# Asking for raw weight tiles a pair ahead in a Strassen-form MLP, and preparing the second product's first blocks in the last pair

## The chip, the cores and the metric

One Trainium2 chip, one core. The metric is device time in microseconds, the time of one execution of the whole kernel. Before the change it is 2197.11 us, the median of three runs (2195.40 to 2198.02).

## The reference

A trunk of two residual mixers (an even and an odd one), each followed by a squared-ReLU MLP, and a last RMSNorm, all in float32, for 1024 tokens of width 1024, with an MLP width of 4096. The change touches the two MLPs alone:

```python
def rmsnorm(x, g):
    xf = x.astype(F32)
    y = xf * lax.rsqrt(jnp.mean(xf * xf, axis=-1, keepdims=True) + EPS)
    return (y * g.astype(F32)).astype(x.dtype)

def sq_relu_mlp(h, w1, w2):
    u = jax.nn.relu(h @ w1)
    return (u * u) @ w2

def reference(x, ...):
    for layer in range(DEPTH):
        ...
        x = x + sq_relu_mlp(rmsnorm(x, norm_mlp[layer]), w_mlp1[layer], w_mlp2[layer])
    return rmsnorm(x, final_norm)
```

## The kernel before

**Precision.** TensorE multiplies reduced float32. Each float32 operand is therefore cut into a high half, a cast by ScalarE (L122), and a low half, the rest, by VectorE (L130), and each product of two blocks is three matmuls: high by high, high by low, low by high. A weight block with its halves is a tile `wb` (1024 columns: 512 high, 512 low); an activation block is `hb`, and in the second product `ub`.

**The first product, h @ w1.** The MLP width is cut into 16 pairs p of two column blocks. A pair needs two raw weight tiles (128 x 1024, 512 KB each), `raw(p, 0)` and `raw(p, 1)`, loaded by SyncE (DMA at L304). The 2 x 2 block product of a pair is computed in Strassen's form (Winograd's variant): 7 products of 12 matmuls (L371, all in `product`) in place of 8. The weight side has the blocks A11, A12, A22 (quarters of raw tiles) and S1 to S4 (sums of quarters, made by GpSimd, L323 to L342); the activation side has B11, B21, B22, t2, t3, T1 and t4 (in `nb.T`, prepared once for each layer by the norm object, from the residual tiles X). A11 needs raw(p, 0) alone, A12 in the first product too, A22 and S1 raw(p, 1), the others both. In what follows a product is named by its pair and activation block: 9t3 is S3 of pair 9 by t3. A11 goes with B11, A12 with B21, A22 with t4, S1 with T1, S2 with t2, S3 with t3, S4 with B22.

**Evacuation.** `head` and `head2` take the products with B11 and B21 out of a PSUM bank (ScalarE, L389, L394, L395), `rest` the other five (VectorE, L400 to L429, and squared ReLU on ScalarE, L375 and L376). The results and their sums for the second product are spilled to DRAM by `put` (SyncE, L382) and read back for the second product at L468. For pairs 14 and 15 (TAIL) the four results are put as they are, without the sums.

**Order of the pairs.** The B blocks of the first token half are ready before those of the second, so pairs 0 to 5 (NS = 6) first do only B11 and B21, from raw(p, 0) alone, while the norm of the second half is worked out: the sum of squares over partitions (L220), the factor on VectorE, its broadcast by TensorE (L231), the scale of X (L1514) and the t and T blocks (`late`, L1526 to L1541, with low halves at L130 and, negated, at L279). Then come the other five products of pairs 0 to 5, whose raw tiles are loaded a second time (both of them, named 16 + p), and then pairs 6 to 15 in full.

**Queues and tiles.** All DMAs are issued by SyncE, in its program order: a DMA whose tile isn't free or whose data isn't ready holds all behind it. A generator (`w_stream`) prepares the weight blocks; the class `Ahead` runs it W_AHEAD = 3 blocks beyond the one in use, and a raw tile is asked for when its first block is prepared. The order of instructions on each engine isn't the source's: the tile framework plans all of them before the kernel is built, and what it decided is shown below in rows. Raw tiles, X, the hb blocks, sums, evacuated halves and reloads share one pool of 41 tiles of 4 KB a partition; `wb` tiles have a pool of eight, four of which are held all through an MLP by weights of the mixer and the tail.

**The second product, u @ w2,** works in three groups of pairs (L484), again with seven products, on blocks from the same generator (raw tiles of w2) and from `t_stream` (reloads `ut`, L468). X is read back at L489 for the residual.

Of the kernel before, what the change touches and what calls it, by code (L numbers as in the profile page):

```python
# [46 lines left out]
class Trunk:  # L47
# [239 lines left out]
            return [x[:, s] for x in two for s in (slice(0, N2), slice(N2, S))]  # L287
        return [self.PB("q"), self.PB("q"), self.PA("q"), self.PA("q")]

    def w_stream(self, l, order, second):  # L290


        nc, a = self.nc, self.a
# [48 lines left out]
                    add(x, x, blk(p, 0, 1), op=ALU.add)  # L342
            return self.block("wb", x)

        for p, b in order:
            yield prep(p, b)

    def first_stream(self, l):

        start = range(NS)  # L350
        order = [x for p in start for x in [(p, "A11")] + [(p - 1, "A12")] * (p > 0)] + [(NS - 1, "A12")]
        order += [(NF // 2 + p, b) for p in start for b in ("S2", "S3", "S1", "A22", "S4")]
        order += [(p, b) for p in range(NS, NF // 2) for b in ("A11", "S2", "S3", "S1", "A12", "A22", "S4")]
        return Ahead(self.w_stream(l, order, False), W_AHEAD)

    def mlp(self, l, nb, nxt, dram):
        nc = self.nc
        dma = nc.sync.dma_start
        V = nc.vector
        NP = NF // 2  # L360
        start = range(NS)
        stream = nb.stream
# [15 lines left out]
        spill = {}  # L378

        def put(p, k, x):  # L380
            d = self.dr.tile([P, N2], F32, tag=f"{dram}{p}{k}", name=f"{dram}{p}{k}")
            dma(d, x)  # L382
            spill[p, k] = d
# [8 lines left out]
        def head2(p, ps, u11):  # L392
            product(ps, nb.T["B21"], False, True)
            nc.scalar.activation(u11, ps, AF.Relu)  # L394
            nc.scalar.activation(u11, u11, AF.Square)  # L395
            put(p, "B11", u11)

        def rest(p, b, c, d, t1, u11, second=None):
# [9 lines left out]
            if second is not None:  # L408
                second()
# [19 lines left out]
            V.tensor_tensor(x4, u21, x2, op=ALU.add)  # L429
            put(p, "t4", x4)  # L430


        early = {}
        for p in start:
# [12 lines left out]
        k = 0  # L447
        for p in start:
            bk = self.banks(k)
            k = 1 - k  # L450
            rest(p, *bk[:3], *early[p][:2])
        for p in range(NS, NP):
            a, b, c, d = self.banks(k)
            k = 1 - k
            t1, u11 = head(p, a)
            rest(p, b, c, d, t1, u11, lambda: head2(p, a, u11))


        products = (("A11", "B11"), ("S1", "T1"), ("A12", "B21"), ("S4", "B22"), ("S3", "t3"), ("S2", "t2"),
                    ("A22", "t4"))  # L460
        seq = [(g, i, p) for g in range(len(GROUPS)) for i in range(7) for p in GROUPS[g]]
        stream = Ahead(self.w_stream(l, [(p, products[i][0]) for g, i, p in seq], True), W_AHEAD)

        def t_stream():
            for g, i, p in seq:
                name = products[i][1]
                x = self.H2("ut", "ut")
                dma(x, spill[p, name])  # L468
                yield self.block("ub", x, neg=(name == "B22"))

        tin = Ahead(t_stream(), W_AHEAD)
        X = [self.G("X") for _ in range(NC)]
        done = nxt(X)
        acc = [self.H2("acv", "acv") for _ in range(4)]
# [1 line left out]

        def second(ps, pairs, first, last):
            for j, p in enumerate(pairs):
                w, x = stream.take(), tin.take()
                for m in range(4):  # L480
                    cs = slice(m * P, (m + 1) * P)
                    lo = slice(N2 + m * P, N2 + (m + 1) * P)
                    for i, (a, b) in enumerate(((w[:, cs], x[:, :N2]), (w[:, cs], x[:, N2:]), (w[:, lo], x[:, :N2]))):
                        nc.tensor.matmul(ps[m], a, b, start=(first and j == 0 and i == 0),  # L484
                                         stop=(j == len(pairs) - 1 and i == 2), skip_group_check=True)
# [5 lines left out]
        for g, pairs in enumerate(GROUPS):  # L491
# [32 lines left out]
            k = 1 - k  # L524
# [1131 lines left out]
GROUPS = (range(0, 5), range(5, 10), range(10, 14))  # L1656
# [5 lines left out]


W_AHEAD = 3

G_BUFS = 41
W_BUFS = 8
# [128 lines left out]
```

## Time and profile before

| | before |
|---|---|
| device time, median of 3 | 2197.11 us (2195.40 to 2198.02) |
| device time of the profiled execution | 2195.6 us |
| its span, first to last instruction | 2193.8 us |
| mean granted clock of TensorE | 0.98 |
| ScalarE busy | 1056.5 us (48%) |
| GpSimd busy | 812.4 us (37%) |
| matmuls of the first product, L371 | 2688, 637.9 us busy, 60.8 us idle before them |
| matmuls of the second product, L484 | 2352, 540.0 us busy, 8.2 us idle before them |

All numbers of the trace are of the profiled execution, in microseconds from its start. In a row of a group, `out<-in` names the tiles without their numbers; behind the bar stand busy time, the mean of one in ns, and the idle time of the engine just before, with what ended most of it. In a row of a timeline stand start, length, engine, line, operation, tiles, count, and in brackets the idle time before it and what ended that. In a list of waits stand the engine and line, what it waited for, the sum in us, the number of waits and the longest. The first product's pairs lie at about 307 to 669 us in the first layer and at 1500 to 1861 us in the second.

### The profile page before, as it was taken

What the parts mean: (1) busy time and instruction counts of PE and PEld (TensorE: products, weight loads), DVE (VectorE), ACT (ScalarE), POOL (GpSimd) and SP (SyncE); (2) the same over time, 40 slices, a digit from 0 to 9 for tenths busy, and PEclk for the clock granted to TensorE, in tenths of its full rate; (3) what the DMA queues carried; (4) which work ended last, traced back from release to release, by engine and by line L of the source; (5) the groups of instructions that cost most, each with busy time, mean ns of one, the idle gap of its engine ahead of it and who ended that gap; (6) DMA issues with size and microseconds to landing.
All of it is one profiled execution on the core that took longest, in us unless ns stands there. A gap on an engine that the chain in (4) does not pass through costs nothing. (4 is left out here: it accounts for less than half of the span.)

```text
span 2193.8 us, 27305 instructions
## 1 busy us (share of the span) xinstructions
PE 2060.6 (94%) x9600; PEld 1687.3 (77%) x9600; DVE 1536.4 (70%) x2365; ACT 1056.5 (48%) x1853; POOL 812.4 (37%) x635
## 2 busy tenths in 40 slices
PE   7999998999999999999997999898999999999997
PEld 5877776677777888888785998786777777788887
DVE  7688757665556877775898888717665555877964
ACT  5247645344444544340565777734544444443423
POOL 4133222232225142242558775462332221523414
PEclk9999998999999999999999999999999999999998
DMA  5630032443447635122112000243343444754402
GB/s 173 158 121 20 20 130 101 164 168 120 158 158 279 209 98 183 58 100 74 34 33 59 11 16 16 77 149 140 110 163 139 159 149 168 264 192 146 143 29 78
DMA packets 115546, 261.34 MB, mean 119 GB/s; under 512 B 19664, under 2 KB 21840, under 8 KB 115408
## 3 DMA queue, kind: packets, MB, share of 16 engines
q1 hardware_dynamic: 115408, 259.59, 35.2%
q8 instruction: 75, 1.23, 0.2%
q14 instruction: 63, 0.52, 0.1%
HBM read 178.28 MB, written 72.35 MB: 114 GB/s over the span
## 5 line engine op out<-in xcount | busy, mean ns | idle before, releaser
L371 PE MATMUL q<-hb,wb 128*128 128x512 f32 x2688 | 637.9, 396 | 60.8 <-ACT wb L122 28.4
L371 PEld LDWEIGHTS q<-hb,wb 128*128 128x128 f32 x2688 | 504.9, 190 | 192.8 <-ACT wb L122 44.8
L484 PE MATMUL q<-ub,wb 128*128 128x512 f32 x2352 | 540.0, 391 | 8.2 <-ACT wb L122 4.6
L484 PEld LDWEIGHTS q<-ub,wb 128*128 128x128 f32 x2352 | 442.8, 189 | 104.8 <-ACT wb L122 6.2
L130 DVE TENSOR_TENSOR wb<-raw,wb 128x512 fp32r<-128x512 f32 x268 | 230.3, 866 | 93.0 <-ACT wb L122 91.9
L122 ACT CAST wb<-raw 128x512 fp32r<-128x512 f32 x268 | 163.7, 618 | 189.9 <-PE q L371 84.3
L327 POOL TENSOR_TENSOR sum<-raw 128x512 f32<-128x512 f32 x32 | 42.1, 1315 | 435.7 <-DMA raw<-in_w_dram 307.2
L130 DVE TENSOR_TENSOR ub<-ut,ub 128x512 fp32r<-128x512 f32 x168 | 137.5, 831 | 71.4 <-ACT ub L122 70.9
L122 ACT CAST ub<-ut 128x512 fp32r<-128x512 f32 x168 | 101.3, 618 | 148.8 <-DVE wb L130 18.3
L130 DVE TENSOR_TENSOR wb<-sum,wb 128x512 fp32r<-128x512 f32 x152 | 127.7, 842 | 38.3 <-ACT wb L122 37.2
L122 ACT CAST wb<-sum 128x512 fp32r<-128x512 f32 x152 | 93.6, 618 | 106.9 <-PE q L371 44.2
L185 PE MATMUL z<-Hh,wh 128*128 128x512 f32 x328 | 129.8, 400 | 9.8 <-ACT wh L122 8.6
L185 PE MATMUL z<-Hl,wh 128*128 128x512 f32 x328 | 130.2, 397 | 3.3 <-DVE Hl L1457 3.1
L245 POOL TENSOR_TENSOR acc<-acc,sq 128x512 f32<-128x512 f32 (+1 forms) x62 | 84.4, 1364 | 126.4 <-ACT sq L244 124.5
L185 PE MATMUL z<-Hh,wl 128*128 128x512 f32 x328 | 129.5, 395 | 0.6 <-DVE wl L130 0.6
L323 POOL TENSOR_TENSOR sum<-raw,raw 128x512 f32<-128x512 f32 x28 | 41.4, 1486 | 209.1 <-DMA raw<-in_w_dram 203.1
L1110 PE MATMUL cav<-cpT,VS 128*128 128x256 f32 x512 | 101.9, 303 | 5.0 <-DVE cpT L1340 2.5
L122 ACT CAST wh<-raw 128x1024 fp32r<-128x1024 f32 (+1 forms) x49 | 49.7, 1015 | 108.9 <-PE z L185 39.4
L1320 PE MATMUL ms<-Kt,Qt 128*128 128x512 f32 (+1 forms) x384 | 99.8, 396 | 2.2 <-ACT e L1327 1.4
L185 PE MATMUL op<-yh,wh 128*128 128x512 f32 x252 | 99.7, 397 | 1.4 <-DVE ya L873 0.9
L185 PE MATMUL op<-yl,wh 128*128 128x512 f32 x252 | 98.8, 393 | 0.0
L185 PE MATMUL op<-yh,wl 128*128 128x512 f32 x252 | 97.9, 393 | 0.0
(343 smaller groups left out, 3798.6 us busy)
## 6 DMA issues: line engine op xcount, KB each, us to landing
raw<-in_w_dram SPq DMA_DIRECT2D x140, 512.0 KB, 4.5
xm<-X SPq DMA_DIRECT2D x32, 256.0 KB, 2.0
X<-xm SPq DMA_DIRECT2D x16, 512.0 KB, 7.0
raw<-in_o_w_out_dram SPq DMA_DIRECT2D x16, 512.0 KB, 3.6
raw<-in_o_w_in_dram SPq DMA_DIRECT2D x11, 512.0 KB, 3.5
raw<-in_e_w_in_dram SPq DMA_DIRECT2D x10, 512.0 KB, 4.9
X<-in_x_dram SPq DMA_DIRECT2D x16, 256.0 KB, 5.7
raw<-in_e_w_out_dram SPq DMA_DIRECT2D x8, 512.0 KB, 3.5
```

Source lines behind the costliest of these rows:

```text
L122: self.nc.scalar.copy(out, x)
L130: e.tensor_tensor(out, x, y, op=ALU.subtract)
L185: self.nc.tensor.matmul(ps, l, r, start=(first and i == 0), stop=(last and i == n - 1))
L245: (eng or nc.gpsimd).tensor_tensor(acc, acc, sq, op=ALU.add)
L323: add(x, blk(p, 1, 0), blk(p, 1, 1), op=ALU.add)
L327: add(s1, blk(p, 1, 0), blk(p, 1, 1), op=ALU.add)
L371: nc.tensor.matmul(ps, a, b, start=(first and c == 0 and i == 0), stop=(c == 3 and i == 2), skip_group_check=True)
L484: nc.tensor.matmul(ps[m], a, b, start=(first and j == 0 and i == 0), stop=(j == len(pairs) - 1 and i == 2), skip_group_check=True)
L1110: nc.tensor.matmul(ACC[0][:, (p % 2) * 256:(p % 2 + 1) * 256], VS[h][:, kb * P:(kb + 1) * P], pp[:, t * N2 + ii * 256:t * N2 + (ii + 1) * ...
L1320: nc.tensor.matmul(ps[:, s], l[rows, qs], r[rows, s], start=(i == 0), stop=(i == 2))
```

## The change

`w_stream` has a new argument `look`. Before it prepares block k, it now asks for the raw tiles that blocks k to k + look need; for the first product look is LOOK = 7, the number of blocks of a pair, and for the second it is 0. The generators of the second product's weight blocks and of its reloads are set up ahead of the pairs, and `turn`, which takes the place of `head2` in pairs 6 to 15, fills both when pair 15 has done its B21. Nothing else is changed. From `product` on, lines stand 5 lines lower in the new file, and from the second product on 12 lower.

```diff
@@ -287,7 +287,7 @@
             return [x[:, s] for x in two for s in (slice(0, N2), slice(N2, S))]
         return [self.PB("q"), self.PB("q"), self.PA("q"), self.PA("q")]
 
-    def w_stream(self, l, order, second):
+    def w_stream(self, l, order, second, look=0):
 
 
         nc, a = self.nc, self.a
@@ -342,7 +342,12 @@
                     add(x, x, blk(p, 0, 1), op=ALU.add)
             return self.block("wb", x)
 
-        for p, b in order:
+        uses = {"A11": (0,), "A12": (1,) if second else (0,), "A22": (1,), "S1": (0, 1) if second else (1,),
+                "S2": (0, 1), "S3": (0,) if second else (0, 1), "S4": (0, 1)}
+        for k, (p, b) in enumerate(order):
+            for q, c in order[k:k + look + 1]:
+                for i in uses[c]:
+                    raw(q, i)
             yield prep(p, b)
 
     def first_stream(self, l):
@@ -351,7 +356,7 @@
         order = [x for p in start for x in [(p, "A11")] + [(p - 1, "A12")] * (p > 0)] + [(NS - 1, "A12")]
         order += [(NF // 2 + p, b) for p in start for b in ("S2", "S3", "S1", "A22", "S4")]
         order += [(p, b) for p in range(NS, NF // 2) for b in ("A11", "S2", "S3", "S1", "A12", "A22", "S4")]
-        return Ahead(self.w_stream(l, order, False), W_AHEAD)
+        return Ahead(self.w_stream(l, order, False, LOOK), W_AHEAD)
 
     def mlp(self, l, nb, nxt, dram):
         nc = self.nc
@@ -429,6 +434,26 @@
             V.tensor_tensor(x4, u21, x2, op=ALU.add)
             put(p, "t4", x4)
 
+        products = (("A11", "B11"), ("S1", "T1"), ("A12", "B21"), ("S4", "B22"), ("S3", "t3"), ("S2", "t2"),
+                    ("A22", "t4"))
+        seq = [(g, i, p) for g in range(len(GROUPS)) for i in range(7) for p in GROUPS[g]]
+        stream2 = Ahead(self.w_stream(l, [(p, products[i][0]) for g, i, p in seq], True), W_AHEAD)
+
+        def t_stream():
+            for g, i, p in seq:
+                name = products[i][1]
+                x = self.H2("ut", "ut")
+                dma(x, spill[p, name])
+                yield self.block("ub", x, neg=(name == "B22"))
+
+        tin = Ahead(t_stream(), W_AHEAD)
+
+        def turn(p, a, u11):
+            head2(p, a, u11)
+            if p == NP - 1:
+                stream2.fill()
+                tin.fill()
+
 
         early = {}
         for p in start:
@@ -453,22 +478,9 @@
             a, b, c, d = self.banks(k)
             k = 1 - k
             t1, u11 = head(p, a)
-            rest(p, b, c, d, t1, u11, lambda: head2(p, a, u11))
-
-
-        products = (("A11", "B11"), ("S1", "T1"), ("A12", "B21"), ("S4", "B22"), ("S3", "t3"), ("S2", "t2"),
-                    ("A22", "t4"))
-        seq = [(g, i, p) for g in range(len(GROUPS)) for i in range(7) for p in GROUPS[g]]
-        stream = Ahead(self.w_stream(l, [(p, products[i][0]) for g, i, p in seq], True), W_AHEAD)
-
-        def t_stream():
-            for g, i, p in seq:
-                name = products[i][1]
-                x = self.H2("ut", "ut")
-                dma(x, spill[p, name])
-                yield self.block("ub", x, neg=(name == "B22"))
-
-        tin = Ahead(t_stream(), W_AHEAD)
+            rest(p, b, c, d, t1, u11, lambda: turn(p, a, u11))
+
+
         X = [self.G("X") for _ in range(NC)]
         done = nxt(X)
         acc = [self.H2("acv", "acv") for _ in range(4)]
@@ -476,7 +488,7 @@
 
         def second(ps, pairs, first, last):
             for j, p in enumerate(pairs):
-                w, x = stream.take(), tin.take()
+                w, x = stream2.take(), tin.take()
                 for m in range(4):
                     cs = slice(m * P, (m + 1) * P)
                     lo = slice(N2 + m * P, N2 + (m + 1) * P)
@@ -1662,6 +1674,7 @@
 
 
 W_AHEAD = 3
+LOOK = 7
 
 G_BUFS = 41
 W_BUFS = 8
```

The instructions of each engine are the same before and after; their order and the slots of their tiles differ. First SyncE at the start of the first layer's MLP, before (`raw` are raw tiles of w1, `xm0` the spill of X, `ut0_0B11` the put of pair 0's B11; the last two raws belong to pairs 3 and 4):

```order
L304 DMA raw_580_2863<-in_w1_dram 128x1024
L304 DMA raw_582_2868<-in_w1_dram 128x1024
L304 DMA raw_585_2876<-in_w1_dram 128x1024
L1491 DMA xm0_91<-X_235_1238 128x512
L1491 DMA xm0_91<-X_234_1237 128x512
L1491 DMA xm0_91<-X_236_1239 128x512
L382 DMA ut0_0B11_3040<-t1_599_2959 128x512
L382 DMA ut0_1B11_3094<-t1_607_2991 128x512
L304 DMA raw_611_3021<-in_w1_dram 128x1024
L304 DMA raw_619_3075<-in_w1_dram 128x1024
```

And after (the first six raws are those of pairs 0 to 5 in their order, the last one is the first of pair 0's second loading):

```order
L304 DMA raw_580_2863<-in_w1_dram 128x1024
L304 DMA raw_581_2865<-in_w1_dram 128x1024
L304 DMA raw_582_2867<-in_w1_dram 128x1024
L304 DMA raw_583_2869<-in_w1_dram 128x1024
L304 DMA raw_584_2871<-in_w1_dram 128x1024
L304 DMA raw_587_2879<-in_w1_dram 128x1024
L1503 DMA xm0_91<-X_235_1238 128x512
L1503 DMA xm0_91<-X_234_1237 128x512
L1503 DMA xm0_91<-X_236_1239 128x512
L387 DMA ut0_0B11_3048<-t1_602_2965 128x512
L387 DMA ut0_1B11_3100<-t1_610_2997 128x512
L304 DMA raw_614_3027<-in_w1_dram 128x1024
```

The raw tiles of pairs 3, 4 and 5, raw_583, raw_584 and raw_587, have moved from behind the put of pair 1's B11 to ahead of the last spills of X.

Next TensorE in the same place, before: the last rows of pair 2's B11, the sum of squares (`ss`) with its broadcast (`ident`, `rr`), then 1B21 (wb_608), 3B11 (wb_612) and 4B11 (wb_620), each of four rows with three matmuls:

```order
L371 MATMUL q_614_3049<-hb_588_2886,wb_586_2878 128x512 x3
L220 MATMUL ss_600_2973<-ones_88,acc_563_2758 128x1 x4
L231 MATMUL q_606_2990<-ident_83,rr_605_2988 128x128 x4
L371 MATMUL q_606_2990<-hb_590_2907,wb_608_2992 128x512 x3
L371 MATMUL q_606_2990<-hb_593_2929,wb_608_2992 128x512 x3
L371 MATMUL q_606_2990<-hb_596_2951,wb_608_2992 128x512 x3
L371 MATMUL q_606_2990<-hb_597_2955,wb_608_2992 128x512 x3
L371 MATMUL q_614_3049<-hb_576_2838,wb_612_3023 128x512 x3
L371 MATMUL q_614_3049<-hb_577_2842,wb_612_3023 128x512 x3
L371 MATMUL q_614_3049<-hb_587_2882,wb_612_3023 128x512 x3
L371 MATMUL q_614_3049<-hb_588_2886,wb_612_3023 128x512 x3
L371 MATMUL q_630_3157<-hb_576_2838,wb_620_3077 128x512 x3
```

And after:

```order
L376 MATMUL q_618_3057<-hb_591_2892,wb_589_2884 128x512 x3
L220 MATMUL ss_603_2979<-ones_88,acc_563_2758 128x1 x4
L376 MATMUL q_632_3161<-hb_576_2838,wb_623_3083 128x512 x3
L376 MATMUL q_632_3161<-hb_577_2842,wb_623_3083 128x512 x3
L376 MATMUL q_632_3161<-hb_590_2888,wb_623_3083 128x512 x3
L376 MATMUL q_632_3161<-hb_591_2892,wb_623_3083 128x512 x3
L231 MATMUL q_609_2996<-ident_83,rr_608_2994 128x128 x4
L376 MATMUL q_609_2996<-hb_593_2913,wb_611_2998 128x512 x3
L376 MATMUL q_609_2996<-hb_596_2935,wb_611_2998 128x512 x3
L376 MATMUL q_609_2996<-hb_599_2957,wb_611_2998 128x512 x3
L376 MATMUL q_609_2996<-hb_600_2961,wb_611_2998 128x512 x3
L376 MATMUL q_644_3222<-hb_576_2838,wb_629_3134 128x512 x3
```

The product 4B11 (wb_623) has moved up between the sum of squares and the broadcast, and 5B11 (wb_629) now comes next after 1B21 (wb_611). In the second layer the broadcast keeps its place ahead of that product.

Last TensorE in the later pairs, before: pair 9's t3 (wb_787), t2 (wb_786) and B21 (wb_794):

```order
L371 MATMUL q_791_4461<-hb_624_3121,wb_787_4428 128x512 x2
L371 MATMUL q_790_4460<-hb_610_3018,wb_786_4407 128x512 x3
L371 MATMUL q_790_4460<-hb_613_3046,wb_786_4407 128x512 x3
L371 MATMUL q_790_4460<-hb_618_3072,wb_786_4407 128x512 x3
L371 MATMUL q_790_4460<-hb_621_3100,wb_786_4407 128x512 x3
L371 MATMUL q_791_4461<-hb_624_3121,wb_787_4428 128x512
L371 MATMUL q_791_4461<-hb_625_3125,wb_787_4428 128x512 x3
L371 MATMUL q_791_4461<-hb_628_3150,wb_787_4428 128x512 x3
L371 MATMUL q_791_4461<-hb_629_3154,wb_787_4428 128x512 x3
L371 MATMUL q_790_4460<-hb_590_2907,wb_794_4479 128x512 x3
L371 MATMUL q_790_4460<-hb_593_2929,wb_794_4479 128x512 x3
```

And after, t3 (wb_789), t2 (wb_788), B21 (wb_796):

```order
L376 MATMUL q_793_4465<-hb_627_3127,wb_789_4432 128x512 x3
L376 MATMUL q_793_4465<-hb_628_3131,wb_789_4432 128x512 x3
L376 MATMUL q_793_4465<-hb_630_3154,wb_789_4432 128x512 x3
L376 MATMUL q_793_4465<-hb_631_3158,wb_789_4432 128x512 x3
L376 MATMUL q_792_4464<-hb_613_3024,wb_788_4411 128x512 x3
L376 MATMUL q_792_4464<-hb_617_3054,wb_788_4411 128x512 x3
L376 MATMUL q_792_4464<-hb_622_3080,wb_788_4411 128x512 x3
L376 MATMUL q_792_4464<-hb_624_3106,wb_788_4411 128x512 x3
L376 MATMUL q_792_4464<-hb_593_2913,wb_796_4483 128x512 x3
L376 MATMUL q_792_4464<-hb_596_2935,wb_796_4483 128x512 x3
```

The product t2 no longer stands inside t3 but behind it, directly ahead of B21. The same holds for the other odd pairs from 9 to 13. On SyncE the two raws that a pair asks for stand where they stood, but they are those of the next pair. At the boundary from the first product to the second the order on SyncE is the same before and after.

## Prediction

> **What bounds the kernel now.** I read the page first, then the list of waits of TensorE, then its timeline where those waits lie, and last the engine or queue that ended each of them.
>
> ```profile
> PE 2060.6 (94%) x9600; PEld 1687.3 (77%) x9600; DVE 1536.4 (70%) x2365; ACT 1056.5 (48%) x1853; POOL 812.4 (37%) x635
> L371 PE MATMUL q<-hb,wb 128*128 128x512 f32 x2688 | 637.9, 396 | 60.8 <-ACT wb L122 28.4
> L327 POOL TENSOR_TENSOR sum<-raw 128x512 f32<-128x512 f32 x32 | 42.1, 1315 | 435.7 <-DMA raw<-in_w_dram 307.2
> raw<-in_w_dram SPq DMA_DIRECT2D x140, 512.0 KB, 4.5
> ```
>
> TensorE is busy 94% of the span, and the change gives it neither more nor fewer matmuls. So the whole question is idle time of TensorE. The matmuls of the first product (L371) have 60.8 us of it over the two layers. A raw weight tile lands 4.5 us after its issue, and GpSimd, whose sums of raw tiles are the head of the preparation (L327), spends 307.2 us waiting for such tiles. That wait costs only where it reaches TensorE:
>
> ```profile
> PE q L371 <- ACT wb L122: 28.4, 14, 8.3
> PE q L371 <- DVE wb L130: 16.6, 17, 3.1
> PE q L371 <- DVE u L403: 6.6, 8, 0.9
> PE q L371 <- DVE t L400: 3.5, 4, 0.9
> ```
>
> 45 of the 60.8 us are waits for a prepared weight block (high half by ScalarE, low half by VectorE). The other 10 are evacuations (L400, L403), which no weight load explains. Where they lie, in TensorE's timeline of the first layer (start, length, matmuls, idle before):
>
> ```profile
> 328.43 1.43 PE L231 MATMUL q<-ident,rr 128*128 128x128 f32 x8 [1.59 <-DVE rr L211]
> 330.54 5.49 PE L371 MATMUL q<-hb,wb 128*128 128x512 f32 x12 [0.67 <-ACT RB L235]
> 342.44 1.22 PE L371 MATMUL q<-hb,wb 128*128 128x512 f32 x2 [6.41 <-ACT wb L122]
> 346.20 28.84 PE L371 MATMUL q<-hb,wb 128*128 128x512 f32 x118 [2.55 <-DVE wb L130]
> ...
> 393.05 6.32 PE L371 MATMUL q<-hb,wb 128*128 128x512 f32 x26 [0.88 <-DVE u L403]
> ...
> 455.21 32.88 PE L371 MATMUL q<-hb,wb 128*128 128x512 f32 x144 [0.88 <-DVE u L403]
> ```
>
> There are three kinds of place: one large hole at the start (342 to 346 us), a broken stretch in pairs 1 to 5 (375 to 461 us), and single waits later. The undisturbed row at 455.21 gives the unit: 144 matmuls in 32.88 us, 0.229 us each, **2.75 us for a product of 12**.
>
> **The start.** SyncE, ScalarE, then the second layer on TensorE:
>
> ```profile
> 337.35 0.32 SPq L382 DMA_DIRECT2D ut_1B<-t  x1
> 337.76 8.62 SPq L304 DMA_DIRECT2D raw<-in_w_dram  x5
> ```
>
> ```profile
> 341.76 1.14 ACT L122 CAST wb<-raw 128x512 fp32r<-128x512 f32 x2 [0.50 <-DMA raw<-in_w_dram]
> ```
>
> ```profile
> 1532.46 1.22 PE L371 MATMUL q<-hb,wb 128*128 128x512 f32 x2 [8.28 <-ACT wb L122]
> 1536.83 21.23 PE L371 MATMUL q<-hb,wb 128*128 128x512 f32 x84 [3.15 <-DVE wb L130]
> ```
>
> SyncE issues in order. The raw tiles of the next pairs stand behind the spill of 1B11, which can't leave before 337.35, so they are issued from 337.76 and the first cast starts at 341.76, when its tile has come. TensorE's idle time is 6.41 + 2.55 = 8.96 us here and 8.28 + 3.15 = 11.43 us in the second layer. In the new order these raws stand ahead of the X spills, well before that put, and their tiles lie on slots long dead. So this wait goes. **What is late next is VectorE**, which carries the norm and the halves of the activations:
>
> ```profile
> 330.52 5.39 DVE L1514 SCALAR_TENSOR_TENSOR X<-X,cols,RB 128x512 f32<-128x512 f32 x8 [2.24 <-ACT RB L235]
> 335.83 2.49 DVE L1526 TENSOR_TENSOR X<-X 128x512 f32<-128x512 f32 x4
> 355.12 7.01 DVE L130 TENSOR_TENSOR hb<-X,hb 128x512 fp32r<-128x512 f32 x6
> 366.27 0.68 DVE L130 TENSOR_TENSOR wb<-sum,wb 128x512 fp32r<-128x512 f32 x1
> ```
>
> From the scale at 330.52 to the low half of product 0t2 (end 366.95) VectorE has 36.4 us of nearly unbroken work. TensorE's own work ahead of 0t2, counted from 336.03, is the 2 matmuls at 342.44 and those from 346.20 to 366.5, 22 us, so it would be there at about 358. VectorE decides. In the new order some 10 low halves of weight blocks leave this chain (they come earlier, while VectorE waits for the norm). A row of it costs 2.49 - 0.69 over three steps, 0.60 us, so 6.0 us go. Against it, pair 4's A11 now stands between the sum of squares and the norm's broadcast: 2.75 us in place of an idle 1.59 us there (the wait L231 on L211), so the norm comes 1.1 us later. 366.95 - 6.0 + 1.1 is about 362: **4 us gained**. In the second layer the broadcast keeps its place; its chain ends so:
>
> ```profile
> 1557.53 0.68 DVE L130 TENSOR_TENSOR wb<-sum,wb 128x512 fp32r<-128x512 f32 x1
> ```
>
> 1558.2 - 6.0 is 1552.2; I take off 0.7 us for a shorter cover of the next block: **5.5 us**. Bounds for both together: a loss of 1.1 (the norm later, and the chain not shortened, since the low halves wait for one of the four turning block tiles), and a gain of 20.4 + 5, the two holes and half of the slow clock in them, if VectorE keeps up. That clock, by windows (length, busy time of PE, PEld, DVE, ACT, POOL, granted clock, DMA):
>
> ```profile
> 339.40:349.60 10.20, 4.61 (x10) 3.22 (x11) 10.20 (x18) 4.68 (x9) 0.00 (x0) 0.50 0.67 244
> 1527.20:1540.80 13.60, 5.19 (x11) 3.64 (x12) 13.60 (x23) 5.01 (x9) 0.00 (x0) 0.50 0.29 112
> 1837.80:1841.20 3.40, 2.98 (x7) 2.40 (x8) 1.57 (x3) 0.42 (x1) 0.00 (x0) 0.50 0.00 0
> ```
>
> I take 9.5 us for the two starts, nearer to the lower end, because the chain of VectorE is in the trace and its cover isn't.
>
> **Pairs 1 to 5.** Two windows, from the end of 0B22 to the end of 5B22 in each layer:
>
> ```profile
> 381.17:460.89 79.72, 71.77 (x302) 55.46 (x302) 48.60 (x71) 32.53 (x55) 23.92 (x19) 1.00 0.46 165
> 1572.83:1652.27 79.44, 71.77 (x301) 55.45 (x302) 48.03 (x71) 32.50 (x55) 24.09 (x19) 1.00 0.46 166
> ```
>
> The work is 25 products, 68.75 us at 2.75. So 11.0 and 10.7 us are lost at waits and restarts. The cause is a raw tile asked for too late:
>
> ```profile
> 393.15 1.29 POOL L327 TENSOR_TENSOR sum<-raw 128x512 f32<-128x512 f32 x1 [9.28 <-DMA raw<-in_w_dram]
> ```
>
> The pair's two raws go out behind the last put of the pair before, and GpSimd stands idle for 9.28 us till they come; all sums, casts and low halves of the pair run late from there. A whole pair ahead (13.75 us here against 4.5 us to land) that wait is covered three times over. What is late then is evacuation: the 0.88 us of L403 is TensorE waiting for a bank that it has just filled itself. By the new order of products I count two such waits left in the five pairs, with 0.2 us of restart each: 2.2 us. **Gain 11.0 - 2.2 = 8.8 us and 10.7 - 2.2 = 8.5 us.** Bounds: half of that, if the waits of L403 stay (eight of up to 0.9 us in both layers, 6.6 in all) and each restarts TensorE, and 11 if none stays; a loss is excluded, since raw tiles can only be asked for as early as before or earlier.
>
> **Pairs 6 to 15.** The rhythm is two pairs:
>
> ```profile
> 523.67 0.73 PE L371 MATMUL q<-hb,wb 128*128 128x512 f32 x2 [1.53 <-ACT wb L122]
> 524.67 38.21 PE L371 MATMUL q<-hb,wb 128*128 128x512 f32 x166 [0.27 <-ACT t L389]
> 564.54 0.73 PE L371 MATMUL q<-hb,wb 128*128 128x512 f32 x2 [1.65 <-ACT wb L122]
> ...
> 653.64 5.68 PE L371 MATMUL q<-hb,wb 128*128 128x512 f32 x24 [0.88 <-DVE t L400]
> ...
> 1836.75 0.74 PE L371 MATMUL q<-hb,wb 128*128 128x512 f32 x2 [1.42 <-ACT wb L122]
> 1838.22 6.67 PE L371 MATMUL q<-hb,wb 128*128 128x512 f32 x22 [0.73 <-DVE wb L130]
> ```
>
> ```profile
> 559.48 1.29 POOL L327 TENSOR_TENSOR sum<-raw 128x512 f32<-128x512 f32 x1 [18.98 <-DMA raw<-in_w_dram]
> ```
>
> 40.87 us for 168 matmuls, 38.5 us of work. The 1.65 us are again the chain raw, sum, cast: the sum starts at 559.48 after 18.98 us of waiting, and TensorE at 564.54. That wait goes, but the new order sets t3, t2, B21 in a row where t2 stood between t3's parts, and there TensorE meets the evacuation L400, as it does already in the last pair (0.88 us), and still the head copy (0.27 us). So a period loses 1.15 + 0.4 of restarts in place of 2.4: 0.8 us, four periods and a like amount in the last pair, **3.4 us in each layer**, and 1.7 us more in the second, where the wait at 1836.75 led into half a clock for 3.4 us. Bounds in a layer: a loss of 5 (the 0.88 comes and the old wait stays, five times), and a gain of 2.4 x 5 = 12.
>
> The Trainium skill, "TensorE: Matmul & The Clock Gate", section "Part 1: The HAM clock gate", lets the clock fall only after an idle window of about 3.4 us. The window at 1837.80 speaks against it: 0.50 right after waits of 1.42 and 0.73 us. By the rule the 1.7 us would have another cause and stay; the sum would then be 33.6 us.
>
> **The prepared blocks in the last pair.** The order of instructions at the boundary is the same before and after on SyncE, so I cost this part at nothing. The wait there:
>
> ```profile
> 690.01 4.61 PE L484 MATMUL q<-ub,wb 128*128 128x512 f32 x12 [2.36 <-ACT wb L122]
> ```
>
> ```profile
> 688.67 0.62 ACT L122 CAST ub<-ut 128x512 fp32r<-128x512 f32 x1 [6.30 <-DMA ut<-ut_3T]
> ```
>
> It hangs on a reload on SyncE that stands behind X loads. Those now have other slots, so it can shrink: at most 2.36 us and half a clock over 3.4 us, 1.7, in each layer, 8 us in all. The ends are 0, as nothing there has changed its place, and 8; I take 0.
>
> **Sum.** 9.5 + 8.8 + 8.5 + 3.4 + 3.4 + 1.7 = 35.3 us. The profiled run took 2195.6 us (span 2193.8), the median of three is 2197.1. 2195.6 - 35.3 = 2160.3, and 1.5 more at the median: **2162 us**.
>
> **Rivals.**
> - Every wait goes, the boundary's too: 8 us more, and VectorE keeps up at the start, 5 more: 2149 to 2154. For it: the slots freed at the boundary. Against it: VectorE's unbroken rows. 0.15.
> - The start gains nothing, because VectorE's chain isn't shortened: 25.8 us, 2171; with half of pairs 1 to 5, 2180. For it: only four block tiles turn, so a block made early has to wait for its tile. 0.20.
> - The requests don't come earlier in time, since a raw tile's slot is free no sooner; only the start's tiles, on dead slots, help: 9.5 us, 2188. For it: the pool of 41 tiles is full in the first product. Against it: no wait of SyncE at L304 is among its ten longest. 0.08.
> - Slower: two more raw tiles live among the 41 tiles of the pool that halves and spills share. A request for a tile that isn't free stops SyncE, and the puts behind it keep their halves, and evacuation stops.
>
> ```profile
> SPq L382 <- ACT u L376: 57.6, 19, 6.0
> ```
>
> From 460 to 660 us SyncE mostly waits for halves to put (this row alone is 57.6 us, the longest 6.0), so a hold of up to 6 us is absorbed. From there on it decides: a wait like the 1.65 us in each of 30 pairs is 49 us, less 35.3: 2211. 0.05. The Trainium skill, "DMA: Bandwidth & Descriptors", section "Anatomy of one DMA", says that a semaphore wait happens on the issuing sequencer before dispatch; the trace agrees, as these waits stand in SyncE's own list.
>
> **How the numbers follow.** Forecast 0.50 (2155 to 2168), the rivals 0.15, 0.20, 0.08 and 0.05, and 0.02 for no change. The range reaches from just under the first rival to just short of the third: 2148 to 2186. A difference under 0.2% (4.4 us) can't be told from none: faster 0.91, same 0.04, slower 0.05.
>
> **What would show it.** At the start, TensorE without the waits of 6 and 8 us on ScalarE, and the low half of 0t2 at about 362 and 1552. In pairs 1 to 5, windows near 71 us and no wait on L130 there; GpSimd's wait for raw tiles far below 307 us, with waits for free tiles in its place. In pairs 6 to 15, periods near 40.0 us. At the boundary the 2.4 us still there. I am wrong if SyncE waits long at L304 (now L309), or if TensorE waits for blocks while their raw tiles lie ready.

## The result, and the profile after

The changed kernel took 2164.47 us, the median of four runs (2162.68 to 2167.30), against 2196.61 us before (2195.40 to 2198.02). The ratio on record is 0.9847, its 95% interval 0.9835 to 0.9859 (the quotient of the two medians is 0.9854): 32 us faster. The forecast was 2162 us. The profiled execution took 2162.68 us, its span is 2160.9, the granted clock 0.986.

The page after, TensorE's busy time, the matmuls of the first product (now L376) and GpSimd's first sum:

```profile
PE 2051.2 (95%) x9600; PEld 1687.6 (78%) x9600; DVE 1546.1 (72%) x2365; ACT 1063.9 (49%) x1853; POOL 833.3 (39%) x635
...
L376 PE MATMUL q<-hb,wb 128*128 128x512 f32 x2688 | 632.0, 395 | 38.0 <-ACT t L394 7.9
...
L327 POOL TENSOR_TENSOR sum<-raw 128x512 f32<-128x512 f32 x32 | 59.4, 1857 | 188.4 <-DVE hb L130 72.4
```

Idle time before the first product's matmuls fell from 60.8 to 38.0 us. GpSimd's idle time before its sums of the first product's pairs (L327) fell from 435.7 us, 307.2 of them for raw tiles, to 188.4, and most of that is now ended by VectorE. But look at the mean: the same 32 sums take 1857 ns each, before it was 1315. Two of them, one at each start, make up most of the difference, as is shown below. TensorE's list of waits after:

```profile
PE q L376 <- ACT t L394: 7.9, 4, 3.0
PE q L376 <- DVE wb L130: 7.8, 5, 2.9
...
PE q L496 <- ACT wb L122: 7.3, 4, 2.7
PE q L376 <- DVE u L408: 6.6, 6, 1.5
PE q L376 <- DVE t L405: 6.5, 8, 0.9
PE q L376 <- ACT wb L122: 3.7, 4, 1.2
```

Waits for a prepared block (the two rows with `wb`) fell from 45.0 to 11.5 us. New is ScalarE's copy of `head`, L394, 7.9 us in four waits. Before, as L389, it was:

```profile
PE q L371 <- ACT t L389: 1.6, 6, 0.3
```

The three stages of the first product, for both layers, are cut from TensorE's timeline: from the second sum of squares (L220) to the end of product 0B22; from there to the end of 5B22; from there to the end of 15B22. (After, 6B11 stands ahead of 5B22; its 2.75 us are counted with the third stage.)

| us, first / second layer | start | pairs 1 to 5 | pairs 6 to 15 |
|---|---|---|---|
| before | 54.6 / 56.8 | 79.7 / 79.4 | 208.6 / 209.4 |
| after | 53.3 / 54.7 | 70.9 / 70.9 | 203.0 / 204.2 |
| gained | 1.3 / 2.2 | 8.8 / 8.5 | 5.6 / 5.2 |
| forecast | 4.0 / 5.5 | 8.8 / 8.5 | 3.4 / 5.1 |

The table gives 31.6 of the 32.9 us between the two profiled executions; the other 1.3 us lie outside the three stages. The windows of pairs 1 to 5 in both layers (with 6B11) and of one period of two later pairs, columns as in the prediction:

```profile
378.62:452.29 73.67, 71.27 (x314) 58.41 (x313) 52.88 (x72) 34.35 (x56) 30.65 (x22) 1.00 0.53 179
1553.42:1627.09 73.67, 71.26 (x314) 58.41 (x313) 52.62 (x72) 34.31 (x56) 31.04 (x22) 1.00 0.52 179
517.34:557.08 39.74, 38.86 (x168) 31.30 (x168) 23.41 (x33) 19.30 (x32) 11.35 (x8) 1.00 0.42 145
```

73.67 - 2.75 is 70.9 us for work of 68.75. A period of two pairs takes 39.74 us, before 40.87.

**The start is where the gain stayed away.** TensorE there, first layer:

```profile
334.61 0.73 PE L376 MATMUL q<-hb,wb 128*128 128x512 f32 x2 [1.19 <-ACT wb L122]
338.23 7.40 PE L376 MATMUL q<-hb,wb 128*128 128x512 f32 x22 [2.88 <-DVE wb L130]
346.73 6.11 PE L376 MATMUL q<-hb,wb 128*128 128x512 f32 x24 [1.10 <-ACT t L394]
353.43 3.01 PE L376 MATMUL q<-hb,wb 128*128 128x512 f32 x12 [0.59 <-ACT t L399]
359.30 12.75 PE L376 MATMUL q<-hb,wb 128*128 128x512 f32 x48 [2.86 <-ACT t L394]
```

The wait for the DMA is gone, and 8.6 us of smaller waits have come for its 9.0. The last one, 2.86 us, stands ahead of 5B21, which in the planned order is the last product before 0t2. Its bank is not free until ScalarE has copied the result of 5B11 out of it (L394). Why that copy is late is read from ScalarE, GpSimd and VectorE in turn:

```profile
358.14 0.62 ACT L122 CAST wb<-sum 128x512 fp32r<-128x512 f32 x1 [4.77 <-POOL sum L328]
358.67 0.58 ACT L394 COPY t<-q 128x512 f32<-128x512 f32 x1
```

```profile
349.14 7.63 POOL L327 TENSOR_TENSOR sum<-raw 128x512 f32<-128x512 f32 x1 [31.20 <-DVE hb L130]
```

```profile
348.92 2.50 DVE L130 TENSOR_TENSOR hb<-X,hb 128x512 fp32r<-128x512 f32 x4
351.33 0.69 DVE L130 TENSOR_TENSOR wb<-raw,wb 128x512 fp32r<-128x512 f32 x1
351.93 3.71 DVE L130 TENSOR_TENSOR hb<-X,hb 128x512 fp32r<-128x512 f32 x6
358.79 1.21 DVE L130 TENSOR_TENSOR wb<-sum,wb 128x512 fp32r<-128x512 f32 x1 [3.16 <-ACT wb L122]
```

ScalarE stands 4.77 us before the cast of 0t2's block, for GpSimd's sum (the cast reads L328, which follows L327), and the copy of 5B11 is queued behind that cast. GpSimd's sum L327, 1.3 us elsewhere, takes 7.63 us: it ends about 1 us after VectorE's unbroken row does (355.6), of which 11 instructions run beside it. What let the sum start at 349.14 was not its raw tile, which had landed at 340.6, but a low half that VectorE ended at 349.0: the sum's tile lies in the slot of the block that this low half read. Before the change, too, a low half of VectorE let the sum start, at 355.89, and its raw tile had landed at 349.2. The second layer shows the same late sum (7.68 us) and the same wait (2.99 us).

### The profile page after: what moved, and what is told of

Same layout as the page of the kernel before. It is cut to its first block, busy times and chain, and to the rows that moved or that the text cites. A ratio compares the mean times of both kernels' runs of the same rounds, so it can differ in the third digit from the quotient of the medians.

```text
span 2160.9 us, 27292 instructions
## 1 busy us (share of the span) xinstructions
PE 2051.2 (95%) x9600; PEld 1687.6 (78%) x9600; DVE 1546.1 (72%) x2365; ACT 1063.9 (49%) x1853; POOL 833.3 (39%) x635
## 5 line engine op out<-in xcount | busy, mean ns | idle before, releaser
L376 PE MATMUL q<-hb,wb 128*128 128x512 f32 x2688 | 632.0, 395 | 38.0 <-ACT t L394 7.9
L376 PEld LDWEIGHTS q<-hb,wb 128*128 128x128 f32 x2688 | 505.3, 190 | 162.7 <-ACT t L394 16.3
L130 DVE TENSOR_TENSOR wb<-sum,wb 128x512 fp32r<-128x512 f32 x152 | 128.8, 849 | 50.6 <-ACT wb L122 49.1
L327 POOL TENSOR_TENSOR sum<-raw 128x512 f32<-128x512 f32 x32 | 59.4, 1857 | 188.4 <-DVE hb L130 72.4
L332 POOL TENSOR_TENSOR raw<-raw,raw 128x512 f32<-128x512 f32 x32 | 42.5, 1329 | 177.0 <-DVE wb L130 160.0
```

Of the source, the lines that this page charges most:

```text
L130: e.tensor_tensor(out, x, y, op=ALU.subtract)
L327: add(s1, blk(p, 1, 0), blk(p, 1, 1), op=ALU.add)
L332: add(x, x, blk(p, 1, 0), op=ALU.add)
L376: nc.tensor.matmul(ps, a, b, start=(first and c == 0 and i == 0), stop=(c == 3 and i == 2), skip_group_check=True)
```

## The experiments

All times are medians with the ratio on record to runs of the kernel before on the same chip, whose median lay between 2197.6 and 2199.7 us in these sessions. These ratios lie up to 0.0012 beside the quotients of the medians. Three pairs of numbers with slashes are the stages in the order of the table, first / second layer.

**One part alone.** Requests ahead without the preparation in the last pair:

```diff
         def turn(p, a, u11):
             head2(p, a, u11)
-            if p == NP - 1:
-                stream2.fill()
-                tin.fill()
```

> Asks for raw tiles a pair ahead as the changed kernel does, but does not prepare blocks of the second product in the last pair. Theory (all of the gain is from the requests; the preparation in the last pair moved nothing): as the changed kernel, 2164.5 us, ratio to before 0.985, and the wait of TensorE at the boundary stays near 2.7 us in each layer. Rival (the second part pays some of it, by the slots it gives at the boundary): 2168 or more, with longer waits at the boundary. A second rival (the preparation is what made the boundary 0.3 to 0.6 us worse in each layer): about 2163.

2165.95 us, ratio 0.9860 (0.9844 to 0.9876). Stages 51.7 / 54.6, 70.9 / 70.9, 203.0 / 204.1. The whole gain is there without the second part; the two ratios' intervals overlap, so the second part is worth nothing that these runs can tell. The start of the first layer differs by 1.5 us between this kernel and the changed one, though nothing there was edited. The difference lies in the clock behind the last wait, in 5B21 (the changed kernel first, then this one; the granted clock is the third number from the end):

```profile
359.30:363.89 4.59, 4.59 (x13) 3.69 (x14) 4.30 (x6) 4.59 (x10) 1.43 (x2) 0.63 0.15 57
362.97:365.99 3.02, 3.02 (x13) 2.52 (x14) 2.73 (x3) 3.02 (x7) 1.45 (x2) 1.00 0.00 0
```

The same product takes 4.59 us at a clock of 0.63 after a wait of 2.86 us, and 3.02 us at 1.00 after one of 2.51. In the second layer both kernels run it at 0.64, after 2.99 and 3.00 us; in the kernel below that asks ahead in the second product too it runs at 1.00 in both layers, after 2.50 and 2.99 us. So a start can come out 1.5 us longer or shorter by the clock alone, and that has to be allowed for in that stage.

The preparation without requests ahead (`LOOK = 0`):

> Only prepares the second product's first blocks in the last pair; raw tiles are asked for as before. Theory: no difference from before, 2196.6 us within 4. Rival (the second part pays): 2193 or less, and the waits at the boundary shrink from 2.36 and 2.05 us.

2207.57 us, ratio 1.0046 (1.0029 to 1.0062): slower than before, which neither theory had. Stages 54.6 / 56.9, **82.8 / 83.7**, 209.7 / 208.4. Pairs 1 to 5 lost 3.1 and 4.3 us, 7.4 of some 10 us. SyncE's request and GpSimd's sum in that kernel, and the request before the change (its sum is the row at 393.15 in the prediction):

```profile
391.19 0.87 SPq L304 DMA_DIRECT2D raw<-in_w_dram  x2
```

```profile
396.25 1.29 POOL L327 TENSOR_TENSOR sum<-raw 128x512 f32<-128x512 f32 x1 [10.26 <-DMA raw<-in_w_dram]
```

```profile
389.08 0.87 SPq L304 DMA_DIRECT2D raw<-in_w_dram  x2
```

From request to sum it is 5.06 us, before it was 4.07. The new list `uses` names raw(p, 0) ahead of raw(p, 1) for S2, where the preparation itself used to touch raw(p, 1) first, the one that the sum reads. In the planned order of SyncE this is all that differs from the kernel before, but for two stores at the very end. To test it, the list was turned round, with `LOOK = 0`:

```diff
-                "S2": (0, 1), ...
+                "S2": (1, 0), ...
```

> As the kernel that only prepares the second product's blocks in the last pair (no requests ahead), which took 2207.6 us, but the two raw tiles of S2 are asked for in the order of before: raw(p, 1), which the first sum reads, then raw(p, 0). Theory (the changed request list asks for raw(p, 0) first, so that the sum's tile comes 1 us later in each of pairs 0 to 5, and that is the loss of pairs 1 to 5, 3.1 and 4.3 us): pairs 1 to 5 back at 79.4 to 79.7 us, about 2199 us. Rival (the preparation in the last pair, or the tiles' new slots, cost it): stays near 2207.

2198.76 us, ratio 1.0003 (0.9993 to 1.0012); pairs 1 to 5 at 77.1 / 76.9, below before, and pairs 6 to 15 at 209.2 / 212.2. In the planned order on SyncE the last put of pairs 1 and 3 now stands behind the two requests that used to follow it, so this isn't quite the kernel before, and that may be why pairs 1 to 5 come out below it. But their loss is gone, as the order of the two requests would have it. In the changed kernel the lead of a pair should hide that order; no run had the lead with the other order.

**The stages apart.** Requests ahead behind the first twelve blocks only, then in the first twelve blocks alone:

```diff
-            for q, c in order[k:k + look + 1]:
+            for q, c in order[k:k + (look if k >= 2 * NS else 0) + 1]:
```

> Asks a pair ahead from the twelfth block on, so in the five later products of pairs 0 to 5 and in pairs 6 to 15; the start's twelve blocks ask as before. Theory (the gains add: 2.6 and 2.2 us at the two starts, 8.8 and 8.5 in pairs 1 to 5, 5.6 and 5.2 in pairs 6 to 15): 28.1 us gained, 2168.5 us, with the start's waits of 6.4 + 2.6 and 8.3 + 3.2 us back. Rival (requests ahead at the start are what lets the later pairs run without waits): 2180 or more, with waits left in pairs 1 to 5.

```diff
-            for q, c in order[k:k + look + 1]:
+            for q, c in order[k:max(k + 1, min(k + look + 1, 2 * NS))]:
```

> Asks ahead in the start's twelve blocks alone, and only for their own tiles. Theory (gains add): 4.7 us gained, 2192 us, with pairs 1 to 5 at 79 to 80 us as before. Rival (it is the second loading of pairs 0 to 5, asked for early, that disturbs the start through GpSimd's sum beside VectorE; without it the start gains what was forecast, 9.5 us): 2187 us, without the 2.9 us waits of TensorE on ScalarE's copy L394.

The first: 2170.30 us, ratio 0.9878 (0.9864 to 0.9893); stages 56.0 / 56.4, 70.9 / 72.5, 203.1 / 203.1. The later stages need no lead at the start. The second: 2196.69 us, 0.9994 (0.9984 to 1.0004); stages **50.6 / 52.0**, 81.9 / 81.7, 211.7 / 208.9. Its start gains 4.0 and 4.8 us, near the forecast of 9.5 for both; pairs 1 to 5 lose 2.2 and 2.3 us, which fits the turned order of their requests, and pairs 6 to 15 of the first layer another 3.1, which was not followed up. The 2.9 us waits on L394 are gone, though the sum does even worse, as its GpSimd and VectorE rows show:

```profile
343.66 18.62 POOL L327 TENSOR_TENSOR sum<-raw 128x512 f32<-128x512 f32 x1 [22.64 <-DMA raw<-in_w_dram]
```

```profile
343.59 1.88 DVE L1545 TENSOR_TENSOR X<-X,X 128x512 f32<-128x512 f32 x3
...
359.85 1.28 DVE L279 SCALAR_TENSOR_TENSOR hb<-X,hb 128x512 fp32r<-128x512 f32 x2
364.30 1.22 DVE L130 TENSOR_TENSOR wb<-sum,wb 128x512 fp32r<-128x512 f32 x1 [3.17 <-ACT wb L122]
```

18.62 us for a sum of 1.3: here it starts when its raw tile lands (343.5), at the head of 29 instructions of VectorE without a gap (0.60 us each, to 361.1), and ends 1.2 us after that row. TensorE then waits for the cast itself:

```profile
364.32 0.73 PE L376 MATMUL q<-hb,wb 128*128 128x512 f32 x2 [2.08 <-ACT wb L122]
```

Here no copy that TensorE needs is queued behind that cast, all products ahead of 0t2 are done by then, and the wait is 2.08 us. So the late sum alone isn't the loss in the changed kernel; it is the late sum with the copy behind its cast.

**How far ahead.** `LOOK = 3`:

> Asks three blocks ahead of the one prepared, in place of seven. Three blocks are some 8 us of products, a raw tile lands in 4 to 5 us. Theory (landing time is what has to be covered, so three are enough in the pairs): pairs 1 to 5 stay at 71 us and pairs 6 to 15 at 203 to 204 us; 2164.5 us within 3. Rival (a request has to get past a whole pair's puts on SyncE, so seven are needed): pairs 1 to 5 lose half of their gain again, 2172 us or more.

2169.94 us, ratio 0.9862 (0.9847 to 0.9876). Pairs 1 to 5 keep their whole gain (70.9 / 71.1), so landing time is covered there by three blocks; pairs 6 to 15 give back 5.0 and 1.4 us (208.0 / 205.6). The interval overlaps with that of seven.

**The sum at the start.** The sums of pair 0's second loading (p is 16 there) made by VectorE:

```diff
         def prep(p, b):
+            add = (nc.vector if p == NF // 2 and not second else nc.gpsimd).tensor_tensor
```

> The sums of the weight blocks of pair 0's second loading are made by VectorE in place of GpSimd; the rest is the changed kernel. Theory (at the start GpSimd's first sum stands still for 6 us beside VectorE's unbroken row, and ScalarE's cast of it holds the copies that TensorE waits for): the 7.6 us sum is gone, the two waits of 2.9 us on L394 with it, the start from the sum of squares to the end of 0B22 falls from 53.3 and 54.7 us to about 50 and 51.5; 6 us gained on the changed kernel, 2158.5 us. Rival (VectorE's own row of work is the bound, and it gets some 2 us more of it): 2164 to 2167.

2153.55 us, ratio **0.9788** (0.9772 to 0.9804), clear of the changed kernel's. The start is 48.1 / 48.8 us, 5.1 and 5.9 below the changed kernel, 11 us where 6 were expected; the other stages are unchanged (70.9 / 70.9, 202.9 / 204.2). About 3 us of the 11 are the clock: behind the waits of 2.86 and 2.99 us, now gone, 5B21 took some 1.5 us longer in each layer. TensorE and VectorE there:

```profile
356.24 6.86 PE L377 MATMUL q<-hb,wb 128*128 128x512 f32 x28 [0.61 <-ACT t L400]
363.32 21.15 PE L377 MATMUL q<-hb,wb 128*128 128x512 f32 x92 [0.23 <-DVE wb L130]
```

```profile
354.15 0.68 DVE L328 TENSOR_TENSOR sum<-raw 128x512 f32<-128x512 f32 x1
```

The sum takes 0.68 us in VectorE's row, and no wait over 0.61 us is left from 356 to 384 us. To learn whether that is worth as much without the requests, the same line in the kernel before:

> The kernel before, without any request ahead, but with the sums of pair 0's second loading on VectorE. Theory (those sums cost TensorE only because requests ahead let them start beside VectorE's unbroken row; before, they took 1.7 us and the 6.4 and 8.3 us waits for raw tiles came first): within 3 us of before, 2197.6 us. Rival (the sums on VectorE are worth their 11 us in any kernel, and have nothing to do with the requests): 2188 or less.

2194.05 us, ratio 0.9976 (0.9962 to 0.9990): a gain of 5 us, more than the 3 allowed for, but half of the 11 in the changed kernel; its start gained 0.9 and 1.8 us (53.7 / 55.0), where the changed kernel's gained 5.1 and 5.9, and pairs 1 to 5 about 1.5 in each layer (78.3 / 77.9). At the start the sum matters mostly together with the requests ahead; why pairs 1 to 5 gained was not followed up.

**One more block tile at the start.** `W_BUFS = 9` and `W_AHEAD = 4` with VectorE's sums:

> Changed kernel, pair 0's second sums on VectorE, and one more block tile (five turn, not four) with a block more prepared ahead. Theory (the waits of 1.19 and 2.9 us for 5B11 at the start are a block that couldn't be cast for want of a tile until after VectorE's scale had begun): they go, start from 48.1 and 48.8 us to about 45, 2147 us against 2153.5. Rival (VectorE's row to the end of the low halves is the bound): 2152 to 2155.

2179.33 us, ratio 0.9907 (0.9892 to 0.9921): some 25 us slower than without. The profiled executions differ by 21.9 us, 9 of them outside the three stages (48.3 / 47.8, 74.5 / 70.8, 211.0 / 206.1); the starts are as long as without. In the first layer the start's waits for 5B11 are gone, but a longer one stands in their place:

```profile
341.06 5.45 PE L377 MATMUL q<-hb,wb 128*128 128x512 f32 x12 [6.79 <-ACT t L395]
```

With a block more prepared ahead, the planned order puts casts ahead of the evacuations that free TensorE's banks (25.1 us of such waits in the whole kernel). What the waits of 1.19 and 2.88 us for 5B11 hang on is not settled by it. In the trace of the changed kernel the cast of that block stands on ScalarE behind the ReLU of 1B21, which starts at 333.45 after 3.11 us of waiting for TensorE, and its low half stands on VectorE behind 11 instructions of the norm, from 330.37 to 337.5; no run moved either.

**The boundary.** The waits there were forecast to stay. They were 2.36 and 2.05 us; after, they are somewhat longer, and a second one stands in the second layer:

```profile
673.45 4.60 PE L496 MATMUL q<-ub,wb 128*128 128x512 f32 x12 [2.74 <-ACT wb L122]
...
1849.34 3.06 PE L496 MATMUL q<-ub,wb 128*128 128x512 f32 x12 [2.66 <-ACT wb L122]
1854.13 12.45 PE L496 MATMUL q<-ub,wb 128*128 128x512 f32 x53 [1.74 <-ACT wb L122]
```

The second product takes the same time all the same: from the end of 15B22 to its last matmul 270.3 us in each layer, before 270.6 and 269.7.

Three attempts on these waits. Requests ahead in the second product too (`look=3` for `stream2`, on the changed kernel):

> The second product's generator also asks ahead, by three blocks. Theory (the waits at the boundary, 2.74 us in the first layer, 2.66 and 1.74 in the second, come from raw tiles asked for behind the X loads): they shrink by half or more, 3 to 6 us gained, 2160 us. Rival (no tile of the pool is free earlier, so SyncE holds the reloads behind a raw tile that can't be placed): 2168 or more.

2164.70 us, ratio 0.9843 (0.9829 to 0.9858): no difference from the changed kernel. The third stage is 2.6 and 2.4 us shorter (200.4 / 201.8), because 16 of the second product's matmuls that stood ahead of the end of 15B22 now stand behind it, and the second product is 4.8 us longer behind that point in the two layers together. A wait of 3.11 us is still there in the first layer.

```profile
679.52 40.86 PE L496 MATMUL q<-ub,wb 128*128 128x512 f32 x167 [3.11 <-ACT wb L122]
```

Sums of the first group on VectorE, in the kernel with VectorE's sums at the start:

```diff
-            add = (nc.vector if p == NF // 2 and not second else nc.gpsimd).tensor_tensor
+            add = (nc.vector if (p in GROUPS[0] and b == "S1" if second else p == NF // 2) else nc.gpsimd).tensor_tensor
```

> Changed kernel, pair 0's second sums on VectorE, and at the boundary the five sums S1 of the second product's first group on VectorE too. Theory (at the boundary GpSimd works without a break for 13.6 us, and the cast that TensorE waits 2.7 us for stands behind its last sum): the waits of 2.5 to 2.7 us there fall under 1 us, 4 to 7 us gained on 2153.5, so 2147 to 2150. Rival (the transfers are the bound, at over 400 GB/s in that stretch): waits stay, 2152 to 2156.

2154.67 us, ratio 0.9794 (0.9777 to 0.9810), the same as with VectorE's sums at the start alone. GpSimd is off the path, and the first wait shrinks (from 2.46 and 2.41 us to 1.67 and 1.07), but ScalarE now stands 5.63 us for a reload, and later waits grow (3.82 us on a reload's low half in the second layer):

```profile
668.75 0.62 ACT L122 CAST ub<-ut 128x512 fp32r<-128x512 f32 x1 [5.63 <-DMA ut<-ut_3T]
```

X read back in halves of its columns, each half later, again with VectorE's sums at the start:

```diff
-        def load(ms):
+        def load(ms, h):
             for m in ms:
-                dma(X[m], nb.spill[m * P:(m + 1) * P, :])
+                dma(X[m][:, h], nb.spill[m * P:(m + 1) * P, h])
...
-                load(range(4, 8))
+                load(range(4, 8), h1)
...
-                load(range(4))
+                load(range(4), h0)
             second(A, pairs, False, True)
+            if g == 0:
+                load(range(4), h1)
...
+            if g == 0:
+                load(range(4, 8), h0)
             A = self.banks(k)
```

> Changed kernel, pair 0's second sums on VectorE, and X read back at the boundary in halves of its columns (256 KB each), each half later, so that 1 MB and not 2 MB stands ahead of the raw tile and the reloads that the first group's last blocks need. Theory (the boundary is bound by the transfers, which run at over 400 GB/s there): the first wait of TensorE at the boundary, 2.46 and 2.41 us, falls under 1.2 us, ratio to before 0.976 against 0.9788. Rival (the reload's own place or GpSimd's sums are the bound): waits and time stay, 0.978 to 0.980.

2154.30 us, ratio 0.9789 (0.9773 to 0.9806): no gain, first waits of 2.79 and 2.15 us. The planned order moved the later halves forward again, so that all of X was still asked for within 21 us, and the stretch is as full as it was:

```profile
665.00:675.00 10.00, 7.21 (x25) 5.21 (x23) 1.99 (x3) 1.76 (x3) 8.39 (x7) 0.83 1.05 397
```

The DMA engines are busy without a gap there (1.05) at 397 GB/s, as they were in the kernel before:

```profile
690.90:694.30 3.40, 3.40 (x10) 2.47 (x8) 1.39 (x2) 0.78 (x2) 3.40 (x3) 0.50 1.05 407
```

That the transfers bound the boundary fits all three attempts, but none took transfers away, so it is argued, not shown.

## Why the prediction was right, and where not

**Where the bound lies** was right: only idle time of TensorE counted, and the time fell by what three stages gave.

**Pairs 1 to 5** came out to a tenth of a microsecond (8.8 and 8.5), and the two evacuation waits that were to be left are there, 0.87 us at 1t4 and 1.52 at 3t4, both at L408. The runs with requests in the later blocks only, or three blocks ahead, keep this gain but for 1.6 us in one layer: it is the landing time of the raw tiles that was covered. That it agrees to a tenth is partly luck. The second of the two waits was 1.52 us and not 0.88, and 32.88 us for 144 matmuls is 0.228 us each, not 0.229, which takes 0.2 us off the work of 25 products.

**The start was mis-sized: 9.5 us forecast, 3.5 measured.** The step was "VectorE decides". VectorE's own chain did what was forecast: from the sum of squares to the low half of 0t2 it took 34.6 and 36.1 us, where the forecast times give 35.4 and 36.2. But the step left out GpSimd and ScalarE. The slot for the sum that 0t2's block needs came free earlier than before, so the sum fell beside VectorE's unbroken row and took 7.63 us; the cast behind it kept the copy waiting that 5B21 needed. So TensorE came to 0t2 only at 363.7, though its block was ready at 360.0. With the sum on VectorE the two starts gained 6.5 and 8.0 us on before, more than was forecast. So the lead on the raw tiles does free the start; most of what it freed was taken by a sum that met VectorE, and by the half clock behind the wait. How much exactly varies: in the two other kernels with the same start, requests alone and requests in the second product too, the starts gained 5.0 and 6.6 us.

**Pairs 6 to 15 were mis-sized the other way: 8.5 us forecast, 10.8 measured.** A part of it is a slip in the sum: 0.8 us in four periods and as much again in the last pair is 4.0 us in a layer, where the prediction added 3.4. By its own terms the forecast is 9.7. For the rest, a period takes 39.74 us in place of the forecast 40.0: the wait at L405 after t2 came as forecast, at 0.78 us and not 0.88, but the 0.27 us for the head copy, forecast to stay, went with the block's wait that it used to follow. The slow clock of the second layer did not come again:

```profile
1800.00:1828.50 28.50, 27.62 (x122) 22.56 (x121) 15.23 (x23) 15.28 (x26) 2.14 (x2) 1.00 0.61 210
```

A lone wait of 1.04 us is left ahead of that stretch, where two of 1.42 and 0.73 had stood; that the 1.7 us hung on those waits fits, but no run put them back alone. Nor did the second layer gain 1.7 us more than the first; it gained 0.4 less, since its waits had been 0.6 us shorter in sum and a new one of 0.85 us for a block came, at 1678.87.

**The second part** was costed at nothing, and is worth nothing. **The boundary** took the same time, as forecast, with its waits a little moved.

**One exclusion was false.** The prediction held a loss in pairs 1 to 5 to be impossible, "since raw tiles can only be asked for as early as before or earlier". The change also turned the order of the two requests round. Without a lead pairs 1 to 5 lost 7.4 us (3.1 and 4.3) by that, and the loss went when the order was turned back. With the lead it showed no harm, but the argument was wrong, and the difference stands in the diff (`uses` against the first line of S2's preparation).

Of the rivals, the one in which SyncE is held by tiles that aren't free did not come: SyncE's waits at L304 (the line kept its number; the prediction has it as L309) add up to some 29 us in the first products of both layers, before to some 31, beside some 250 us of waits to put in each layer. The rival in which the start gains little was near to what happened at the start, but by another mechanism: VectorE's chain was shortened, and one more block tile left the starts as they were and made the rest slower.

The best version seen is the changed kernel with pair 0's second sums on VectorE: 0.9788 of before.

## What to carry to other kernels

When a wait for a transfer is taken away, follow its data one step further than the engine that was next in the trace: here the wait for it was replaced by a sum that started earlier and met another engine's busiest stretch. A request list written out beside the code that uses the tiles has an order of its own; put first what is read first. An evacuation queued behind a cast waits for whatever the cast waits for, so more preparation ahead can cost more than it gives.

## What the hardware showed unexpectedly

GpSimd's sum of 1.3 us stood still here as long as VectorE ran without a gap. At the start before the change it took 1.68 us, with VectorE slowed to 1.17 us an instruction on average (the row at 355.12 in the prediction, beside three instructions of GpSimd):

```profile
355.89 1.68 POOL L327 TENSOR_TENSOR sum<-raw 128x512 f32<-128x512 f32 x1 [37.58 <-DVE hb L130]
```

Beside 11 instructions of VectorE at full speed it took 7.63 us, beside 29 of them 18.62. In the last two GpSimd ended about 1.15 us, nearly its own length, after VectorE's row. The Trainium skill, "SBUF — State Buffer", section "SBUF: two separate sides", says that VectorE and GpSimd share one port pair by an exclusive lock, held for one instruction, while the other blocks. The trace agrees that one blocks, but it blocked for a whole row of instructions and not for one. Why the same sum was let in between VectorE's instructions before, and not after, is open.
